# Moving GpSimd's two-tensor instructions to VectorE, and one causal selection for all heads, in a hybrid SSD and short-convolution layer

## The chip, the cores and the metric

The kernel runs on one core of one Trainium2 chip. The metric is the device time of one execution in microseconds; the runs shown are medians of several executions. In the profile PE is the matrix engine (TensorE) and PEld its weight loads, DVE is VectorE, ACT is ScalarE, POOL is GpSimd, and SP is the engine whose queue issues all of this kernel's data DMAs.

## The reference, cut to what matters

One layer on x of 2048 tokens by 1024, in float32:

```python
h = rmsnorm(x, norm_pre)
xbc, dt_raw, z_ssd, sc_h, sc_b, sc_c, z_sc = jnp.split(h @ w_in, idx, axis=-1)
xbc = silu(causal_dwconv(xbc, ssd_conv_w, ssd_conv_b))      # xs, B, C
dt = softplus(dt_raw + dt_bias)
# chunked scan, 16 chunks of 128 tokens, 16 heads in 2 groups
decay_in = exp(segsum(dt * a))                 # exp(acs_l - acs_s) for s <= l, else 0
y_diag = einsum(einsum(C, B) * decay_in, xd)   # C.B^T is shared by a group's 8 heads
states = einsum(B, xd * decay_states)
y_ssd = y_diag + y_off + d_skip * xs
y_ssd = rmsnorm_by_group(y_ssd * silu(z_ssd))
y_sc = sc_b * causal_dwconv(sc_c * sc_h, sc_conv_w) * silu(z_sc)
x = x + rmsnorm(concat(y_ssd, y_sc) @ w_out, norm_post)
out = x + sigmoid(x @ w_ple_gate) * (p @ w_ple_proj)
```

## The kernel before, in words

Everything is kept transposed: channels on the 128 partitions, tokens along the free dimension. The tokens are worked on in two blocks of 1024 (b = 0, 1), each in halves of 512. Precision comes from a split: each float32 operand of a matmul becomes a rounded part (a copy on ACT, L138 for weights and L203 for activations) and the remainder (a subtraction, L139 for weights on VectorE, L204 for activations), and three matmuls stand for one product.

The program has three stages.

**Projection (to about 1069 us).** The input projection is done by a seven-product scheme of the Winograd/Strassen kind (class `Wino`): the weights of two column tiles and the activations of two token halves are added and subtracted first, and seven products p = 1 to 7 take the place of eight. The sums of the weights (`wino_pieces`, L178, L179, L181, L187: tiles `wr_*`) are made on GpSimd. The sums of the activations (`refill`) are made on VectorE or, for some, GpSimd. `Weights.fill` keeps up to six split weight tiles (`ws_*`) ready ahead of PE. Results leave PSUM through ACT (L315) and VectorE (L593, L627, L649, L659, L678); the short convolution's gate ends with two products on GpSimd (L692, L693, tile `vs`). Each block has 13 groups of tiles; from group to group the loads of raw weights (`wr_*`, nine buffers) run ahead.

**Heads (about 1069 to 1384 us).** Eight pairs of head tiles. For a pair: the tokens-by-channels form `px` is made by transposes on PE, multiplied by dt on VectorE (L889, tile `xd`), and that by the decay to the chunk's end on GpSimd (L890, tile `xdd`); the chunk states `pst` need `xdd` (L910). For each of four heads a mask tile `m` (128 x 1024) is filled with the cumulated decays by a broadcast DMA (`m<-acs_d`); GpSimd writes -1e30 where l < s (L936, an affine selection), ACT takes eight exponentials (L939), and VectorE multiplies by `gsb` = C.B^T/4, the same tile for all heads of a group (L941). PE uses the products in `py` (L966) and fills up with matmuls of the second half of the output projection (`os`, L828), 768 in all, dealt out evenly over the steps.

**Output (from about 1384 us).** `out_proj` (PE tile `mo`), post-norm and residual (`residual`: L1080 scales on VectorE, L1081 adds x on GpSimd), then the gate (`mg`, L1104 to L1107). Steps of the norms and of the operands are hung on numbered units by a plan.

The order of the instructions on each engine is fixed when the program is built: a scheduler lays out the instructions by estimated times, so that a change of an engine also changes places on the others. Each engine then takes its own list strictly in order and waits where an operand is late. VectorE makes a part of every split operand and also empties PSUM, so PE can wait for it in two ways.

The lines that the change touches:

```python
G.tensor_tensor(s["e"], s["c"], s["d"], ALU.add)                     # L178, weight sums
(eng or V).tensor_tensor(a[:, 1, :], src, a[:, 0, :].bitcast(F32), ALU.subtract)   # L204
G.tensor_tensor(r4(xdd[gr]), r4(xd[gr]), bc(dst[b]), ALU.mult)       # L890
G.affine_select(m, m, pattern=[[0, NCH], [1, CH]], compare_op=ALU.is_ge, fill=-1e30, ...)   # L936
V.tensor_tensor(mf, mf, s["gsb"][gr], ALU.mult)                      # L941
G.tensor_tensor(x2[d + i], x2[d + i], xk[:, i, :], ALU.add)          # L1081
```

Of the kernel before, what the change touches and what calls it, by code (L numbers as in the profile page):

```python
# [60 lines left out]
def hybrid_kernel(ctx: ExitStack, tc: tile.TileContext, xT, pT, w_t, w_dt, w_o, w_g, w_p, cols_d, cst_d, outT):  # L61
# [99 lines left out]
    def wino_pieces(src, order, pairs, nkk, name, pool):  # L161
# [7 lines left out]
        def fill(p, pr, kk):  # L169
            def f(sp):  # L170
# [4 lines left out]
                elif p == 5:  # L175
                    s["c"], s["d"] = raw(pr, kk, 1, 0), raw(pr, kk, 1, 1)
                    s["e"] = pool.tile([P, 4, P], F32, tag="wraw", name=f"wr_{name}_{label(pr)}_e{kk}")
                    G.tensor_tensor(s["e"], s["c"], s["d"], ALU.add)  # L178
# [21 lines left out]
    def split_act(src, name, p, eng=None, pool=None):  # L200
# [3 lines left out]
        (eng or V).tensor_tensor(a[:, 1, :], src, a[:, 0, :].bitcast(F32), ALU.subtract)  # L204
        return a
# [1002 lines left out]
```

## Time and profile before

| what | value |
|---|---|
| median of 3 runs | 1769.39 us (1767.48 to 1770.1) |
| the profiled execution | 1771.42 us, its span 1769.2 us |
| mean granted PE clock | 0.987 |
| ACT busy | 779.2 us (44%) |
| HBM | 147 GB/s over the span |

The page of a profile gives each engine's busy time; the windows view gives it for stretches that are named; the waits view says which engine stood idle for whom; the timeline lists instructions with their start and length, and in brackets the idle time ahead of one and who ended it. In the profile's instruction names the running numbers of the tiles are left out. Matmul ends are modelled, so PE's busy share is read as "had work", and the rest of a stretch is time in which PE certainly stood.

### The profile page before, as it was taken

Reading aid. Unit: us, or ns where it says so; the run is one execution under the profiler, and the core shown is the slowest. Engines: PE = TensorE matmul, PEld = TensorE weight load, DVE = VectorE, ACT = ScalarE, POOL = GpSimd, SP = SyncE. Lnnn points to the kernel's source line nnn. Section 1 sums busy time; section 2 is a strip of 40 time slices with the busy share of each in tenths; the row PEclk is TensorE's granted clock in tenths of the full one; section 3 lists DMA queues with packets and bytes.
Section 4 is the critical chain, followed back from the end, with each engine's and each line's share of the span. In section 5 each row is a group of like instructions: output and inputs, shape, how many; then the busy total and the mean of one; then the engine's idle time right before and its main releaser. Section 6 shows DMA issues by size and latency. Waiting matters only on the chain. (4 is left out here: it accounts for less than half of the span.)

```text
span 1769.2 us, 23037 instructions
## 1 busy us (share of the span) xinstructions
PE 1678.1 (95%) x8324; PEld 1360.4 (77%) x8324; DVE 1254.9 (71%) x1500; ACT 779.2 (44%) x1408; POOL 627.9 (35%) x450
## 2 busy tenths in 40 slices
PE   7989999989999999999999999998889898998998
PEld 5768878878888788788888887776677686787886
DVE  7986766797669876577766685687578638579632
ACT  7563444435336434344444365455645324152421
POOL 0454243353445543433324443245333104335200
PEclk9999999999999999999999999999999999999999
DMA  9362222673225413221232248687787735435432
GB/s 311 134 202 68 93 83 66 229 250 122 67 66 195 133 60 107 69 84 66 96 107 85 66 155 275 213 262 252 232 261 229 238 105 164 145 119 180 135 119 84
DMA packets 122693, 262.28 MB, mean 148 GB/s; under 512 B 17098, under 2 KB 19658, under 8 KB 121556
## 3 DMA queue, kind: packets, MB, share of 16 engines
q1 hardware_dynamic: 122580, 260.83, 44.9%
q8 instruction: 65, 1.06, 0.3%
q14 instruction: 48, 0.39, 0.1%
HBM read 192.45 MB, written 68.33 MB: 147 GB/s over the span
## 5 line engine op out<-in xcount | busy, mean ns | idle before, releaser
L828 PE MATMUL os<-act_m,ws_os 128*128 128x512 f32 x768 | 191.8, 402 | 3.8 <-ACT po L832 3.2
L214 PE MATMUL mo<-act_m,ws_o 128*128 128x512 f32 x768 | 182.2, 397 | 12.6 <-DVE x L1059 12.6
L214 PE MATMUL mg<-act_x2s,ws_g 128*128 128x512 f32 x768 | 178.5, 394 | 5.8 <-ACT gth L1104 5.8
L214 PEld LDWEIGHTS mo<-act_m,ws_o 128*128 128x128 f32 x768 | 144.8, 190 | 49.9 <-DVE x L1059 12.8
L828 PEld LDWEIGHTS os<-act_m,ws_os 128*128 128x128 f32 x768 | 142.8, 191 | 42.1 <-issue 8.3
L214 PEld LDWEIGHTS mg<-act_x2s,ws_g 128*128 128x128 f32 x768 | 144.1, 189 | 40.0 <-ACT gth L1104 9.8
L139 DVE TENSOR_TENSOR ws_A_gb<-wr_A_gb,ws_A_gb 128x512 fp32r<-128x512 f32 x96 | 89.4, 931 | 35.6 <-ACT ws_A_gb L138 35.4
L204 POOL TENSOR_TENSOR act_m<-mraw,act_m 128x512 fp32r<-128x512 f32 x32 | 53.9, 1688 | 146.9 <-ACT act_m L203 82.7
L138 ACT CAST ws_A_gb<-wr_A_gb 128x512 fp32r<-128x512 f32 x96 | 59.7, 622 | 68.7 <-POOL wr_A_gb L187 20.6
L139 DVE TENSOR_TENSOR ws_A_gc<-wr_A_gc,ws_A_gc 128x512 fp32r<-128x512 f32 x96 | 76.8, 800 | 15.4 <-ACT ws_A_gc L138 14.8
L939 ACT ACTIVATE m<-m,adt 128x128 f32<-128x128 f32 x256 | 77.4, 390 | 16.8 <-POOL m L936 16.8
L606 DVE SCALAR_TENSOR_TENSOR xo<-ux,cols,xo 128x1024 f32<-128x1024 f32 x60 | 80.5, 1344 | 4.5 <-ACT xo L602 4.2
L138 ACT CAST ws_A_gc<-wr_A_gc 128x512 fp32r<-128x512 f32 x96 | 59.8, 623 | 52.7 <-PE A_gc5X L311 8.3
L178 POOL TENSOR_TENSOR wr_A_gc_e<-wr_A_gc,wr_A_gc 128x512 f32<-128x512 f32 x16 | 26.3, 1641 | 138.4 <-DMA wr_A_gc<-in_w_t_dram 119.0
L1105 DVE SCALAR_TENSOR_TENSOR gth<-gth,pe 128x512 f32<-128x512 f32 x32 | 27.5, 859 | 66.8 <-ACT gth L1104 66.8
L1081 POOL TENSOR_TENSOR x<-x,xres 128x512 f32<-128x512 f32 x32 | 50.6, 1600 | 48.8 <-DMA xres<-in_xT_dram 28.5
L1104 ACT ACTIVATE gth<-mg 128x512 f32<-128x512 f32 x32 | 19.1, 598 | 105.4 <-PE mg L214 90.7
L139 DVE TENSOR_TENSOR ws_A_z<-wr_A_z,ws_A_z 128x512 fp32r<-128x512 f32 x48 | 48.2, 1003 | 21.9 <-ACT ws_A_z L138 21.9
L187 POOL TENSOR_TENSOR wr_A_gc<-wr_A_gc,wr_A_gc 128x512 f32<-128x512 f32 x16 | 25.3, 1583 | 103.3 <-DVE ws_A_gc L139 101.4
L936 POOL TENSOR_SCALAR_AFFINE_SELECT m<-m 128x1024 f32<-128x1024 f32 x32 | 47.0, 1478 | 42.2 <-DMA m<-acs_d 41.9
L214 PE MATMUL A_ple<-act_p,ws_p 128*128 128x512 f32 x192 | 49.4, 415 | 11.3 <-ACT ws_p L138 9.1
L890 POOL TENSOR_TENSOR xdd<-xd,dst 128x1024 f32<-128x1024 f32 x16 | 40.3, 2519 | 54.8 <-DVE xd L889 54.8
(504 smaller groups left out, 4070.2 us busy)
## 6 DMA issues: line engine op xcount, KB each, us to landing
wr_A_gc<-in_w_t_dram SPq DMA_DIRECT2D x64, 256.0 KB
wr_A_gb<-in_w_t_dram SPq DMA_DIRECT2D x64, 256.0 KB
m<-acs_d SPq DMA_DIRECT2D x32, 512.0 KB
ple_d<-A_pe SPq DMA_DIRECT2D x32, 256.0 KB
wr_A_xs<-in_w_t_dram SPq DMA_DIRECT2D x32, 256.0 KB
ysc_d<-vs SPq DMA_DIRECT2D x16, 512.0 KB
wr_A_z<-in_w_t_dram SPq DMA_DIRECT2D x32, 256.0 KB
xs_d<-xo SPq DMA_DIRECT2D x16, 512.0 KB
```

The costliest lines, as they stand in the source:

```text
L138: S.copy(sp[:, 0, :kn, :], raw[:, :kn, :])
L139: V.tensor_tensor(sp[:, 1, :kn, :], raw[:, :kn, :], sp[:, 0, :kn, :].bitcast(F32), ALU.subtract)
L178: G.tensor_tensor(s["e"], s["c"], s["d"], ALU.add)
L204: (eng or V).tensor_tensor(a[:, 1, :], src, a[:, 0, :].bitcast(F32), ALU.subtract)
L214: TE.matmul(out, sp[:, a, (k0 + k) % 4, :], act[k0 + k][:, b, :], start=k0 + k == 0 and q == 0, stop=k0 + k == n - 1 and q == 2)
L606: V.scalar_tensor_tensor(o, u[:, q:q + TB], col(w0 + q), o, ALU.mult, ALU.add)
L828: TE.matmul(ps, sp[:, a, k, :], acts_o[tg][KD + kk][:, b_, :], start=kk == 0 and n == 0, stop=kk == KD - 1 and n == 2)
L890: G.tensor_tensor(r4(xdd[gr]), r4(xd[gr]), bc(dst[b]), ALU.mult)
L936: G.affine_select(m, m, pattern=[[0, NCH], [1, CH]], compare_op=ALU.is_ge, fill=-1e30, base=0, channel_multiplier=-1)
L939: S.activation(m[:, c, :], m[:, c, :], AF.Exp, bias=nacs[b][:, h, c:c + 1])
L1081: G.tensor_tensor(x2[d + i], x2[d + i], xk[:, i, :], ALU.add)
L1105: V.scalar_tensor_tensor(th, th, 1.0, pe, ALU.add, ALU.mult)
```

## The change

Every two-tensor instruction that GpSimd did (343: 327 of 128 x 512, 16 of 128 x 1024) is issued on VectorE instead. The 32 selections on the mask tiles are gone. In their place GpSimd selects on `gsb` once per group and block (4 in all), with fill 0, right after ACT has written it; the exponentials then also cover the entries above the diagonal, and the product on VectorE bounds each decay by 1 ahead of the multiplication, in the same instruction. What stays on GpSimd are memsets, small copies and those 4 selections.

```diff
@@ wino_pieces
-                    G.tensor_tensor(s["e"], s["c"], s["d"], ALU.add)
-                    G.tensor_tensor(s["c"], s["c"], s["a"], ALU.subtract)
+                    V.tensor_tensor(s["e"], s["c"], s["d"], ALU.add)
+                    V.tensor_tensor(s["c"], s["c"], s["a"], ALU.subtract)
                     split_w(sp, s["e"])
-                    G.tensor_tensor(s["a"], s["a"], s["e"], ALU.subtract)
+                    V.tensor_tensor(s["a"], s["a"], s["e"], ALU.subtract)
...
-                    G.tensor_tensor(s["a"], s["b"], s["a"], ALU.add)
+                    V.tensor_tensor(s["a"], s["b"], s["a"], ALU.add)
@@ split_act
-        (eng or V).tensor_tensor(a[:, 1, :], src, a[:, 0, :].bitcast(F32), ALU.subtract)
+        V.tensor_tensor(a[:, 1, :], src, a[:, 0, :].bitcast(F32), ALU.subtract)
@@ Wino.refill (and so for p = 6, 7, 4)
-                    e = G if k % 2 and p not in on_v else V
...
-                        e.tensor_tensor(src, t1, t0, ALU.subtract)
+                        V.tensor_tensor(src, t1, t0, ALU.subtract)
@@ prepare
-                G.tensor_tensor(p7, t[:, 1, :], u[:, 1, :], ALU.subtract)
+                V.tensor_tensor(p7, t[:, 1, :], u[:, 1, :], ALU.subtract)
@@ ShortOut.take
-                G.tensor_tensor(v[:, TG:], v[:, TG:], blk[1, 1], ALU.mult)
-                G.tensor_tensor(v[:, :TG], v[:, :TG], z0, ALU.mult)
+                V.tensor_tensor(v[:, TG:], v[:, TG:], blk[1, 1], ALU.mult)
+                V.tensor_tensor(v[:, :TG], v[:, :TG], z0, ALU.mult)
@@ step_g
                     S.activation(s["gsb"][gr], pg[gr], AF.Copy, scale=0.25)
+                    g3 = s["gsb"][gr].rearrange("p (c l) -> p c l", c=NCH)
+                    G.affine_select(g3, g3, pattern=[[0, NCH], [1, CH]], compare_op=ALU.is_ge, fill=0.0, base=0,
+                                    channel_multiplier=-1)
@@ transposes
-                    G.tensor_tensor(r4(xdd[gr]), r4(xd[gr]), bc(dst[b]), ALU.mult)
+                    V.tensor_tensor(r4(xdd[gr]), r4(xd[gr]), bc(dst[b]), ALU.mult)
@@ mask
-                    G.affine_select(m, m, pattern=[[0, NCH], [1, CH]], compare_op=ALU.is_ge, fill=-1e30,
-                                    base=0, channel_multiplier=-1)
                     for c in range(NCH):
                         S.activation(m[:, c, :], m[:, c, :], AF.Exp, bias=nacs[b][:, h, c:c + 1])
                     mf = m.rearrange("p c l -> p (c l)")
-                    V.tensor_tensor(mf, mf, s["gsb"][gr], ALU.mult)
+                    V.scalar_tensor_tensor(mf, mf, 1.0, s["gsb"][gr], ALU.min, ALU.mult)
@@ residual
-                G.tensor_tensor(x2[d + i], x2[d + i], xk[:, i, :], ALU.add)
+                V.tensor_tensor(x2[d + i], x2[d + i], xk[:, i, :], ALU.add)
```

All callers of `split_act` lose their engine argument (`refill`, `p_input`, `later_input`, `mixes_ahead`, `mix_pair`, `operands`). Line numbers of the changed kernel differ by up to two from those before.

How the instructions stand in three places. The last number of a tile's name is a running number and differs between the two programs; the rest is the same tile.

**The heads, third pair.** VectorE before, from the second `ssum` of a pair to the weight splits behind the next pair's masks:

```order
L976 TENSOR_TENSOR ssum_8502<-ssum_8502,gz_9016 128x1024
L941 TENSOR_TENSOR m_9239<-m_9239,gsb_8498 128x1024
L889 TENSOR_TENSOR xd_9329<-px_9320,dts_104 128x1024
L941 TENSOR_TENSOR m_9241<-m_9241,gsb_8498 128x1024
L139 TENSOR_TENSOR ws_os_7_3_9453<-wr_os_7_3_9454,ws_os_7_3_9453 128x512
L139 TENSOR_TENSOR ws_os_0_2_9458<-wr_os_0_2_9459,ws_os_0_2_9458 128x512
```

GpSimd before, at the same place:

```order
L890 TENSOR_TENSOR xdd_9259<-xd_9258,dst_108 128x1024
L936 AFFINE_SELECT m_9239<-m_9239 128x1024
L936 AFFINE_SELECT m_9241<-m_9241 128x1024
L890 TENSOR_TENSOR xdd_9330<-xd_9329,dst_108 128x1024
L936 AFFINE_SELECT m_9308<-m_9308 128x1024
L936 AFFINE_SELECT m_9310<-m_9310 128x1024
```

VectorE with the change:

```order
L977 TENSOR_TENSOR ssum_8502<-ssum_8502,gz_9006 128x1024
L942 SCALAR_TENSOR_TENSOR m_9217<-m_9217,gsb_8498 128x1024
L891 TENSOR_TENSOR xd_9307<-px_9298,dts_104 128x1024
L942 SCALAR_TENSOR_TENSOR m_9219<-m_9219,gsb_8498 128x1024
L892 TENSOR_TENSOR xdd_9308<-xd_9307,dst_108 128x1024
L139 TENSOR_TENSOR ws_os_7_3_9422<-wr_os_7_3_9423,ws_os_7_3_9422 128x512
L139 TENSOR_TENSOR ws_os_0_2_9427<-wr_os_0_2_9428,ws_os_0_2_9427 128x512
```

The selections are gone, and `xdd` stands on VectorE behind `xd`, with one mask product between them. Of the eight pairs' second `xdd`, five stand behind such a product, two behind a weight split, one directly behind `xd`.

**A group's weight sums, projection, first block, after head tiles 2 and 6.** GpSimd before:

```order
L178 TENSOR_TENSOR wr_A_gc_e_3336<-wr_A_gc_100_3332,wr_A_gc_110_3334 128x512
L179 TENSOR_TENSOR wr_A_gc_100_3332<-wr_A_gc_100_3332,wr_A_gc_000_3284 128x512
L604 COPY halo_x<-ux_2_3245 128x3
L178 TENSOR_TENSOR wr_A_gb_e_3364<-wr_A_gb_100_3360,wr_A_gb_110_3362 128x512
L179 TENSOR_TENSOR wr_A_gb_100_3360<-wr_A_gb_100_3360,wr_A_gb_000_3304 128x512
L604 COPY halo_x<-ux_6_3280 128x3
L181 TENSOR_TENSOR wr_A_gc_000_3284<-wr_A_gc_000_3284,wr_A_gc_e_3336 128x512
L181 TENSOR_TENSOR wr_A_gb_000_3304<-wr_A_gb_000_3304,wr_A_gb_e_3364 128x512
L187 TENSOR_TENSOR wr_A_gc_000_3284<-wr_A_gc_010_3465,wr_A_gc_000_3284 128x512
L187 TENSOR_TENSOR wr_A_gb_000_3304<-wr_A_gb_010_3486,wr_A_gb_000_3304 128x512
```

VectorE before, where the results of that group leave PSUM (`ux`, `zo`):

```order
L593 TENSOR_TENSOR ux_2_3245<-A_xs2Z,A_xs_6_3211 128x512
L139 TENSOR_TENSOR ws_A_xs_4_0_3248<-wr_A_xs_110_3011,ws_A_xs_4_0_3248 128x512
L627 TENSOR_TENSOR zo_2_3263<-A_z2Z,A_z_6_3228 128x512
L139 TENSOR_TENSOR ws_A_z_4_0_3265<-wr_A_z_110_3035,ws_A_z_4_0_3265 128x512
L593 TENSOR_TENSOR ux_6_3280<-A_xs2X,A_xs_5_3176 128x512
L139 TENSOR_TENSOR ws_A_gc_1_0_3283<-wr_A_gc_000_3284,ws_A_gc_1_0_3283 128x512
L627 TENSOR_TENSOR zo_6_3300<-A_z2X,A_z_5_3194 128x512
L139 TENSOR_TENSOR ws_A_gb_1_0_3303<-wr_A_gb_000_3304,ws_A_gb_1_0_3303 128x512
```

VectorE with the change:

```order
L139 TENSOR_TENSOR ws_A_xs_4_0_3248<-wr_A_xs_110_3011,ws_A_xs_4_0_3248 128x512
L178 TENSOR_TENSOR wr_A_gb_e_3364<-wr_A_gb_100_3360,wr_A_gb_110_3362 128x512
L179 TENSOR_TENSOR wr_A_gb_100_3360<-wr_A_gb_100_3360,wr_A_gb_000_3304 128x512
L625 TENSOR_TENSOR zo_2_3263<-A_z2Z,A_z_6_3228 128x512
L139 TENSOR_TENSOR ws_A_z_4_0_3265<-wr_A_z_110_3035,ws_A_z_4_0_3265 128x512
L591 TENSOR_TENSOR ux_6_3280<-A_xs2X,A_xs_5_3176 128x512
L139 TENSOR_TENSOR ws_A_gc_1_0_3283<-wr_A_gc_000_3284,ws_A_gc_1_0_3283 128x512
L181 TENSOR_TENSOR wr_A_gc_000_3284<-wr_A_gc_000_3284,wr_A_gc_e_3336 128x512
L625 TENSOR_TENSOR zo_6_3300<-A_z2X,A_z_5_3194 128x512
L139 TENSOR_TENSOR ws_A_gb_1_0_3303<-wr_A_gb_000_3304,ws_A_gb_1_0_3303 128x512
L181 TENSOR_TENSOR wr_A_gb_000_3304<-wr_A_gb_000_3304,wr_A_gb_e_3364 128x512
```

The sums of `wr_A_gb` (which need two loaded raw tiles) now stand in VectorE's list ahead of `zo_2`, the result of PE's tile `A_z2Z`.

**The output stage, between the second reciprocal and the result of `mo_2`.** VectorE before:

```order
L1074 RECIPROCAL rs_1_12213<-rs_1_12213 128x512
L139 TENSOR_TENSOR ws_o_4_0_12264<-wr_o_4_0_12265,ws_o_4_0_12264 128x512
L1080 SCALAR_TENSOR_TENSOR x_0_6_11914<-x_0_6_11914,cols,rs_0_12131 128x512
L1059 TENSOR_TENSOR x_3_1_12240<-mo_0_12179,part_0_12180 128x512
L139 TENSOR_TENSOR ws_o_4_1_12269<-wr_o_4_1_12270,ws_o_4_1_12269 128x512
L1080 SCALAR_TENSOR_TENSOR x_0_7_11949<-x_0_7_11949,cols,rs_0_12131 128x512
L1065 TENSOR_TENSOR ssq_3_12068<-ssq_3_12068,sq_3_1_12242 128x512
L1080 SCALAR_TENSOR_TENSOR x_1_0_11551<-x_1_0_11551,cols,rs_1_12213 128x512
L1080 SCALAR_TENSOR_TENSOR x_1_1_11578<-x_1_1_11578,cols,rs_1_12213 128x512
L1080 SCALAR_TENSOR_TENSOR x_1_2_11691<-x_1_2_11691,cols,rs_1_12213 128x512
L1080 SCALAR_TENSOR_TENSOR x_1_3_11720<-x_1_3_11720,cols,rs_1_12213 128x512
L1059 TENSOR_TENSOR x_2_2_12298<-mo_2_12251,part_2_12252 128x512
```

VectorE with the change:

```order
L139 TENSOR_TENSOR ws_o_3_0_12162<-wr_o_3_0_12163,ws_o_3_0_12162 128x512
L139 TENSOR_TENSOR ws_o_3_1_12167<-wr_o_3_1_12168,ws_o_3_1_12167 128x512
L1081 SCALAR_TENSOR_TENSOR x_0_2_11538<-x_0_2_11538,cols,rs_0_12039 128x512
L1081 SCALAR_TENSOR_TENSOR x_0_3_11567<-x_0_3_11567,cols,rs_0_12039 128x512
L1082 TENSOR_TENSOR x_0_2_11538<-x_0_2_11538,xres_2_12157 128x512
L1082 TENSOR_TENSOR x_0_3_11567<-x_0_3_11567,xres_2_12157 128x512
L139 TENSOR_TENSOR ws_o_4_0_12172<-wr_o_4_0_12173,ws_o_4_0_12172 128x512
L1081 SCALAR_TENSOR_TENSOR x_0_4_11680<-x_0_4_11680,cols,rs_0_12039 128x512
L1081 SCALAR_TENSOR_TENSOR x_0_5_11709<-x_0_5_11709,cols,rs_0_12039 128x512
L1060 TENSOR_TENSOR x_3_1_12148<-mo_0_12087,part_0_12088 128x512
L139 TENSOR_TENSOR ws_o_4_1_12177<-wr_o_4_1_12178,ws_o_4_1_12177 128x512
L1060 TENSOR_TENSOR x_2_2_12206<-mo_2_12159,part_2_12160 128x512
```

The second fence begins three rows behind the reciprocal; in these three stand the result `x_3_0` and one more L1082. Between the reciprocal and the result of `mo_2` stood six scalings (L1080); now four scalings (L1081) and three residual adds (L1082, which were GpSimd's) stand there, and the other scalings come later.

More of the change, by code (lines that the diff above doesn't have):

```diff
@@ L257, in tmp, with refill @@
             return self.pc.tile([P, self.n], F32, tag="wc", name=f"{self.part}_{name}")
-        def refill(self, acts, name, order, l1, l2, on_v=()):
+        def refill(self, acts, name, order, l1, l2):
             h1, h2 = {}, {}
@@ L280, in refill @@
                         src = t0
-                        e.tensor_tensor(src, t0, h2[k, 1], ALU.subtract)
+                        V.tensor_tensor(src, t0, h2[k, 1], ALU.subtract)
                     elif p == 3:
@@ L285, in refill @@
                         src = t1
-                        e.tensor_tensor(src, t1, h2[k, 1], ALU.subtract)
+                        V.tensor_tensor(src, t1, h2[k, 1], ALU.subtract)
                     else:
                         src = h2[k, 0]
-                        e.tensor_tensor(src, src, t0, ALU.add)
-                    acts[p].append(split_act(src, f"{self.part}{name}_{p}{k}", p, e, pact if p in FIRST else self.pactx))
+                        V.tensor_tensor(src, src, t0, ALU.add)
+                    acts[p].append(split_act(src, f"{self.part}{name}_{p}{k}", p, pact if p in FIRST else self.pactx))
                 yield
@@ L420, in p_input @@
                     W.fill(2 * (tg + 1))
-                pa[tg] = [split_act(raws[k], f"p_{tg}{k}", p, None, None if p in FIRST else A.pactx) for k in range(2)]
+                pa[tg] = [split_act(raws[k], f"p_{tg}{k}", p, None if p in FIRST else A.pactx) for k in range(2)]
             for tg in AHEAD:
@@ L450, in l2 @@
                 return h2[k, half]
-            for n, _ in enumerate(A.refill(acts[0], "0", ORDER0, l1, l2, FIRST + (2, 7))):
+            for n, _ in enumerate(A.refill(acts[0], "0", ORDER0, l1, l2)):
                 if 2 <= n < 6:
@@ L501, in later_input @@
                     for i in range(2):
-                        acts[b][p].append(split_act(t[:, i, :], f"A{b}_{p}{k + i}", p, G if k + i == 3 else V,
+                        acts[b][p].append(split_act(t[:, i, :], f"A{b}_{p}{k + i}", p,
                                                     pact if p in FIRST else A.pactx))
@@ L513, in mixes_ahead @@
                     for i in range(2):
-                        acts_o[tg][k + i] = split_act(t[:, i, :], f"m_{tg}_{k + i}", FIRST[2 * tg + (k - KD) // 4],
-                                                      G if i else V)
+                        acts_o[tg][k + i] = split_act(t[:, i, :], f"m_{tg}_{k + i}", FIRST[2 * tg + (k - KD) // 4])
                     if k % 4:
@@ L788, in mix_pair @@
                                        ALU.mult, ALU.mult)
-            acts_o[tg][k + i] = split_act(raw[:, i, :], f"m_{tg}_{k + i}", FIRST[2 * (tg % 2) + k % KD // 4], G if i else V)
+            acts_o[tg][k + i] = split_act(raw[:, i, :], f"m_{tg}_{k + i}", FIRST[2 * (tg % 2) + k % KD // 4])
     def ssd_bank(name):
```

5 lines of the change are left out of this document (2 added, 3 removed).

## The prediction

> **What bounds the kernel now.** I read the page's engine shares first, then a windows view cut where PE's idle time lies, then PE's waits.
>
> ```profile
> PE 1678.1 (95%) x8324; PEld 1360.4 (77%) x8324; DVE 1254.9 (71%) x1500; ACT 779.2 (44%) x1408; POOL 627.9 (35%) x450
> ...
> 37.00:105.00 68.00, 56.73 (x237) 44.78 (x236) 65.21 (x82) 41.32 (x80) 31.96 (x18) 0.95 0.56 187
> ...
> 340.00:400.00 60.00, 54.31 (x235) 43.33 (x234) 54.24 (x56) 25.53 (x42) 28.26 (x19) 1.00 0.72 245
> 400.00:565.00 165.00, 165.00 (x732) 136.45 (x731) 120.25 (x136) 79.15 (x131) 67.03 (x50) 1.00 0.32 106
> 565.00:600.00 35.00, 30.57 (x125) 23.82 (x124) 31.88 (x33) 17.01 (x32) 21.63 (x15) 0.95 0.54 176
> ...
> 1069.00:1384.00 315.00, 283.88 (x2278) 224.43 (x2276) 226.67 (x290) 167.72 (x384) 116.82 (x71) 0.97 0.76 245
> ...
> 1455.00:1520.00 65.00, 53.93 (x223) 42.25 (x222) 56.79 (x63) 21.20 (x35) 24.82 (x16) 0.96 0.51 165
> ...
> 1580.00:1625.00 45.00, 39.87 (x171) 31.70 (x170) 43.98 (x38) 16.45 (x23) 26.56 (x17) 1.00 0.52 164
> ```
>
> A row has the stretch, its length, then busy time and count of PE, PEld, DVE, ACT and POOL, then the granted clock, DMA share and GB/s. PE is the bound over the whole: 1769.2 less 1678.1 leaves 91 us in which it stood. From 400 to 565 it never stands, so nothing on VectorE can gain there, though VectorE has 27% free. PE stands where VectorE is full: in 37:105 VectorE is busy 96%, in 340:400 90%, in 565:600 91%, in 1455:1520 87%, in 1580:1625 98%. PE's idle time there is 11.3 + 5.7 + 4.4 + 11.1 + 5.1 = 37.6 us. In the heads (1069:1384) PE stands 31.1 us with VectorE at 72%: there it is a chain.
>
> ```profile
> PE pst L910 <- POOL xdd L890: 15.1, 8, 5.1
> PE mo L214 <- DVE x L1059: 12.6, 5, 4.1
> ...
> PE A_gc0X L311 <- DVE A_gc L649: 6.7, 1, 6.7
> PE pn L230 <- DVE ssum L976: 6.7, 2, 5.4
> PE mg L214 <- ACT gth L1104: 5.8, 2, 5.1
> ```
>
> PE's waits (total, times, longest) agree: half of the heads' idle time is the eight waits for GpSimd's `xdd`, and in the full stretches PE waits for a PSUM bank that VectorE has not yet emptied.
>
> **Term 1: VectorE's own instructions, with GpSimd beside them and without.** Two engines over the same 6 us of the output stage, where VectorE always has the next instruction ready:
>
> ```profile
> 1490.94 0.68 DVE L1059 TENSOR_TENSOR x<-mo,part 128x512 f32<-128x512 f32 x1
> 1491.55 0.67 DVE L204 TENSOR_TENSOR act_m<-mraw,act_m 128x512 fp32r<-128x512 f32 x1
> 1492.14 1.77 DVE L1080 SCALAR_TENSOR_TENSOR x<-x,cols,rs 128x512 f32<-128x512 f32 x1
> 1493.84 0.68 DVE L1065 TENSOR_TENSOR ssq<-ssq,sq 128x512 f32<-128x512 f32 x1
> 1494.44 1.78 DVE L1080 SCALAR_TENSOR_TENSOR x<-x,cols,rs 128x512 f32<-128x512 f32 x1
> 1496.14 0.68 DVE L139 TENSOR_TENSOR ws_o<-wr_o,ws_o 128x512 fp32r<-128x512 f32 x1
> ...
> 1493.99 1.67 POOL L1081 TENSOR_TENSOR x<-x,xres 128x512 f32<-128x512 f32 x1 [0.63 <-DVE x L1080]
> 1496.30 1.64 POOL L1081 TENSOR_TENSOR x<-x,xres 128x512 f32<-128x512 f32 x1 [0.63 <-DVE x L1080]
> ```
>
> From start to start an undisturbed 128x512 takes VectorE 0.60 us (1491.55 to 1492.14, 1493.84 to 1494.44). The L1080 that runs beside a GpSimd instruction takes 1.70 us (1494.44 to 1496.14). So a GpSimd instruction that meets one of VectorE's costs it 1.1 us, and the same work done by VectorE itself costs 0.60.
>
> By the Trainium skill (SBUF — State Buffer, Who interferes with whom) a VectorE instruction with two SBUF inputs and a GpSimd instruction that reads SBUF exclude each other, and the second waits until the first is done. The trace agrees: 1.70 against 0.60 us.
>
> Not every GpSimd instruction meets one, so I work each full stretch out: VectorE's count there at 0.60 us, plus GpSimd's count (all taken as moved) at 0.60, against the busy time. The reciprocals stand apart:
>
> ```profile
> L1074 DVE RECIPROCAL rs<-rs 128x512 f32<-128x512 f32 x4 | 13.4, 3342 | 0.6 <-ACT rs L1073 0.6
> ```
>
> Two of these four lie in each of the last two stretches (by their timelines). 37:105: 82 x 0.60 + 18 x 0.60 = 60.0, against 65.2: -5.2. 1455:1520: 61 x 0.60 + 6.7 + 16 x 0.60 = 52.9, against 56.8: -3.9. 1580:1625: 36 x 0.60 + 6.7 + 17 x 0.60 = 38.5, against 44.0: -5.5. These three lose 14.6 of 166.0 us, 9%. 340:400 and 565:600 hold 1024-wide instructions as well; at the same 9% of 54.2 + 31.9 they lose 7.6. VectorE's lists in the full stretches become 22 us shorter, though it does more. Not all of PE's idle time there is VectorE's, and a shortened list shows the next cause (ACT, a DMA), so I take two thirds: **-15 us**. The bounds are nothing and all of the 37.6.
>
> In the output stage the order helps too: the adds come off GpSimd's 1.6 us, and the result of `mo_2`, for which PE stands, is moved ahead of two scalings of the other half. That lies within the term.
>
> **Term 2: the heads.** The third pair's second tile, on three engines:
>
> ```profile
> 1165.73 1.22 DVE L889 TENSOR_TENSOR xd<-px,dts 128x1024 f32<-128x1024 f32 x1
> 1166.93 1.23 DVE L941 TENSOR_TENSOR m<-m,gsb 128x1024 f32<-128x1024 f32 x1
> 1168.07 3.92 DVE L139 TENSOR_TENSOR ws_os<-wr_os,ws_os 128x512 fp32r<-128x512 f32 x2
> ...
> 1167.10 2.85 POOL L890 TENSOR_TENSOR xdd<-xd,dst 128x1024 f32<-128x1024 f32 x1 [4.84 <-DVE xd L889]
> ...
> 1170.00 1.20 PE L910 MATMUL pst<-xdd,btok 128*64 128x128 f32 x18 [1.60 <-POOL xdd L890]
> ...
> L936 POOL TENSOR_SCALAR_AFFINE_SELECT m<-m 128x1024 f32<-128x1024 f32 x32 | 47.0, 1478 | 42.2 <-DMA m<-acs_d 41.9
> ...
> L927 DVE SCALAR_TENSOR_TENSOR ea<-ct,ea 128x1024 f32<-128x1024 f32 x16 | 18.8, 1214 | 0.0
> ```
>
> `xd` ends at 1166.95 and PE gets `xdd` at 1170.0, 3.05 later. Changed, one mask product (1.14 from start to start, 1166.93 to 1168.07) and `xdd` at the price of `xd` (1.22) stand there: 2.4, so 0.65 less. Where `xdd` follows `xd` directly it saves 1.6. Ahead of it the chain has the mask, whose product stands in front of `xd` in VectorE's list: without a selection of 1.48 us its exponentials start sooner, though a mask whose DMA lands last gains no more than that. I take 1.1 us of gain for each of the eight waits, together **-9 us**, held by the 15.1 that PE waits for `xdd`. The rest of the 31.1 (loads at a DMA share of 0.76, the `ssum` at the end) I leave as it is. What is late next in this chain is ACT's exponentials and the mask's DMA.
>
> The product with a bound is a form that the trace has only without the bound (L927, 1214 ns mean at 1024 wide, against 1.22 above): nothing either way. The four selections on `gsb` stand several steps ahead of their first reader: nothing; uncovered, 1.48 each, 6 us at the most.
>
> **Term 3: waits that VectorE takes over.** GpSimd stood for data that VectorE now asks for:
>
> ```profile
> POOL wr_A_gc_e L178 <- DMA wr_A_gc<-in_w_t_dram: 119.0, 11, 45.5
> ...
> POOL wr_A_xs_e L178 <- DMA wr_A_xs<-in_w_t_dram: 45.4, 7, 11.0
> ...
> POOL x L1081 <- DMA xres<-in_xT_dram: 28.5, 6, 6.5
> ...
> 403.74 0.68 DVE L627 TENSOR_TENSOR zo<-A_z2Z,A_z 128x512 f32<-128x512 f32 x1
> ...
> 407.04 1.29 POOL L178 TENSOR_TENSOR wr_A_gb_e<-wr_A_gb,wr_A_gb 128x512 f32<-128x512 f32 x1 [1.47 <-DMA wr_A_gb<-in_w_t_dram]
> ```
>
> Most of that is GpSimd being early. But in the changed order the sum of `wr_A_gb` stands ahead of `zo<-A_z2Z`, which ran at 403.74, while its data came at 407.0: VectorE would stand 3.3 us with a PSUM result behind it, then two such results and three weight splits. Such a wait delays PE only if a bank is wanted back within that time; a product of 12 matmuls takes PE 2.7 us (732 in 165 us), eight banks serve it, and six weight tiles lie ready (16 us). I take **+3 us** for the whole. The bounds are nothing, and 20 if half of some 14 groups pass 3 us on to PE.
>
> **The sum.** -15 - 9 + 3 = -21 us. The profiled execution took 1771.4 (span 1769.2), 2 above the median of the runs, 1769.4. So the changed kernel's median is 1748. SP's queue issues the same DMAs, on it only neighbours change places.
>
> **Rivals.**
>
> *Nothing moves (1769, from 1766 to 1773).* PE's idle time is set by ACT and the DMAs, and what VectorE gains becomes their wait. For it: in the heads the DMAs are 76% busy, and the wait for `mg` is put down to ACT. Against it: ACT is 33 to 61% busy in the five full stretches (16.45 of 45 us counts as 37, 21.20 of 65 as 33, 41.32 of 68 as 61), and `mo` and `A_gc0X` wait for VectorE itself.
>
> *VectorE's list is blocked by loads (1780; from 1773 to 1790).* The mechanism of term 3 in the projection, where PE has no slack to give (165.0 of 165): 14 groups x 3.3 us = 46 us of standing VectorE, of which half reaches PE, +23, and with half of the gains, -12: 1769 + 11 = 1780. It decides once a wait is longer than the reserve of a bank, about 5 us (two products). For it: the 119 us row. Against it: VectorE has 45 of 165 us free there.
>
> *VectorE does not become faster (1795).* If its long instructions were long for another reason, the 85 moved instructions of the five stretches (18 + 19 + 15 + 16 + 17) would add 51 us at 0.60 to lists with 3 + 6 + 3 + 8 + 1 = 21 us free: +30, less 4 in the heads. The pairs of 0.68 and 1.78 us above speak clearly against it.
>
> The Trainium skill (Perfetto Trace Analysis, Optimizing Scalar/DVE Operations) advises the opposite for a saturated VectorE, to offload to GpSimd, and adds that between these two it might not help. By the advice this rival's time would come out; the measured 1.70 against 0.60 us decides for the caution.
>
> *More comes free (1730).* All idle time of the full stretches goes (-37.6) and term 2 holds, with term 3 nothing.
>
> **Chances.** The forecast (1735 to 1764) 0.60; more 0.10; nothing moves 0.14; blocked by loads 0.11; not faster 0.05. Some 0.2% (3.5 us) is what a measurement of this kernel can tell from no change. Faster by more: 0.60 + 0.10 = 0.70; same: 0.14; slower: 0.11 + 0.05 = 0.16. The range leaves out the blocked and the not faster case and the far end of "more": 1727 to 1774.
>
> **What would show it.** Term 1: L1080's successor near 0.7 us mean, VectorE's total within 3% of 1255 us despite 343 more instructions, and PE's idle time in the full stretches halved. Term 2: PE's wait for `xdd` below 7 us. Term 3: VectorE's waits for `wr_*` loads under 40 us, with PE still unbroken in the projection. It is wrong if VectorE's total rises by 100 us or more, or if PE waits in the projection where it did not.

## The result, and the profile after

| | before | changed | ratio (95%) |
|---|---|---|---|
| median | 1768.83 us | 1697.48 us (1696.41 to 1702.38) | 0.9602 (0.9582 to 0.9622) |
| span of the profiled execution | 1769.2 us | 1694.7 us | |
| mean granted PE clock | 0.987 | 0.996 | |

The kernel became 4.0% faster, by 71 us. Forecast were 21, and the time lies 30 us below the range's low end of 1727: the sign was right, the size was not.

The page of the changed kernel, engine shares, and below them its windows view. The stretches begin and end with the same matmuls as those shown of before (columns as there; the two stretches that end at 543.20 and 1037.20 answer to 400:565 and to 600:1069):

```profile
PE 1658.7 (98%) x8324; PEld 1351.9 (80%) x8324; DVE 1255.4 (74%) x1843; ACT 783.5 (46%) x1408; POOL 45.6 (3%) x79
```

```profile
37.00:95.70 58.70, 56.84 (x242) 45.75 (x241) 57.40 (x93) 39.37 (x75) 0.00 (x0) 0.98 0.56 185
...
325.40:378.20 52.80, 52.80 (x234) 43.72 (x233) 48.94 (x69) 27.29 (x44) 0.88 (x4) 1.00 0.78 256
378.20:543.20 165.00, 165.00 (x731) 136.50 (x730) 128.96 (x181) 80.41 (x132) 4.08 (x11) 1.00 0.34 116
543.20:571.10 27.90, 27.90 (x124) 23.09 (x123) 25.77 (x41) 16.36 (x28) 7.11 (x2) 1.00 0.62 205
571.10:1037.20 466.10, 466.10 (x2066) 385.91 (x2065) 347.54 (x501) 204.76 (x332) 15.86 (x20) 1.00 0.28 94
1037.20:1326.90 289.70, 276.98 (x2278) 219.94 (x2276) 216.11 (x319) 165.61 (x381) 7.04 (x12) 0.99 0.82 266
...
1399.20:1452.10 52.90, 51.93 (x223) 41.20 (x223) 46.64 (x66) 21.44 (x35) 0.00 (x0) 1.00 0.54 179
...
1512.40:1552.10 39.70, 39.70 (x172) 31.69 (x172) 36.31 (x50) 16.59 (x23) 0.00 (x0) 1.00 0.60 191
```

Three things are to be seen. VectorE does 343 instructions more in the same busy time (1255.4 after 1254.9): what it took over is as much as what it no longer lost. The five full stretches became 41 us shorter (273 to 232), and PE's idle time in them fell from 37.6 to 2.8 us. And PE's busy time fell too, by 19.4 us, though it does the same 8324 matmuls.

The span lost 74.5 us: 34.8 of PE's idle time in the full stretches, 18.4 in the heads (31.1 to 12.7), 1.9 elsewhere, and 19.4 of PE's busy time. The last term is one that the prediction did not have. PE's waits in the changed kernel:

```profile
PE pn L230 <- DVE ssum L977: 4.7, 2, 3.8
PE mo L214 <- DVE x L1060: 4.3, 4, 1.7
...
PE pst L912 <- DVE xdd L892: 0.4, 1, 0.4
```

The 15.1 us for `xdd` are 0.4, the 12.6 for `mo` 4.3, and the 6.7 for `A_gc0X` are gone.

Where PE's busy time went is seen in the kernel before, at a long stand of the output stage. Windows of before; the granted clock is the first number behind POOL's busy time and count:

```profile
1512.20:1516.40 4.20, 0.16 (x1) 0.00 (x0) 4.20 (x6) 0.02 (x1) 2.73 (x2) 0.87 0.74 250
1516.40:1518.00 1.60, 1.56 (x4) 1.31 (x5) 1.60 (x3) 0.61 (x1) 0.41 (x1) 0.50 0.04 8
1518.00:1520.00 2.00, 2.00 (x7) 1.51 (x6) 1.95 (x4) 0.00 (x0) 0.00 (x0) 0.50 0.76 253
1520.00:1522.00 2.00, 2.00 (x6) 1.61 (x5) 0.00 (x0) 0.00 (x0) 1.38 (x2) 0.50 0.01 3
1522.00:1524.00 2.00, 2.00 (x10) 1.56 (x10) 0.00 (x0) 0.00 (x0) 1.14 (x1) 0.96 0.00 0
```

PE stands 4.2 us, and then runs at clock 0.50 for 5.6 us: 17 matmuls start in them, which at the later pace of 10 in 2 us would take 3.4. So this stand cost more than 6 us and not 4.2. In the mean clock: 1769.2 x 0.013 is 23.0 us, 1694.7 x 0.004 is 6.8, a difference of 16.2 of the 19.4, as an estimate.

### The profile page after: what moved, and what is told of

It is laid out like the page before. It is cut to its first block, busy times and chain, and to the rows that moved or that the text cites. A ratio compares the mean times of both kernels' runs of the same rounds, so it can differ in the third digit from the quotient of the medians.

```text
span 1694.7 us, 22635 instructions
## 1 busy us (share of the span) xinstructions
PE 1658.7 (98%) x8324; PEld 1351.9 (80%) x8324; DVE 1255.4 (74%) x1843; ACT 783.5 (46%) x1408; POOL 45.6 (3%) x79
## 4 chain that ended last, share of the span: by engine, by line
PE 85%; DMA 6%; DVE 6%; ACT 2%; issue 1%; SPq 0%; DVEq 0%; ACTq 0%
PE mg L214 10%; PE mo L214 8%; PE os L826 6%; PE py L967 1%; PE A_xs1X L310 1%; PE A_gc6X L310 1%; PE A_gc7X L310 1%; PE A_gb6X L310 1%; PE A_z3X L310 1%; PE A_xs3X L310 1%; PE A_gc5X L310 1%; PE A_z2X L310 1%; PE A_xs2X L310 1%; PE A_gb4X L310 1%; PE A_gc4X L310 1%; PE A_gc3X L310 1%
## 5 line engine op out<-in xcount | busy, mean ns | idle before, releaser
L826 PE MATMUL os<-act_m,ws_os 128*128 128x512 f32 x768 | 186.0, 396 | 2.4 <-ACT po L830 1.7
L826 PEld LDWEIGHTS os<-act_m,ws_os 128*128 128x128 f32 x768 | 141.2, 188 | 37.6 <-issue 6.6
L139 DVE TENSOR_TENSOR ws_A_gb<-wr_A_gb,ws_A_gb 128x512 fp32r<-128x512 f32 x96 | 65.8, 686 | 33.0 <-ACT ws_A_gb L138 32.9
L139 DVE TENSOR_TENSOR ws_A_gc<-wr_A_gc,ws_A_gc 128x512 fp32r<-128x512 f32 x96 | 66.0, 687 | 14.1 <-ACT ws_A_gc L138 12.8
L942 DVE SCALAR_TENSOR_TENSOR m<-m,gsb 128x1024 f32<-128x1024 f32 x32 | 39.6, 1246 | 19.1 <-ACT m L939 16.8
L214 PEld LDWEIGHTS A_ple<-act_p,ws_p 128*128 128x128 f32 x192 | 37.4, 196 | 18.7 <-ACT ws_p L138 9.0
L139 DVE TENSOR_TENSOR ws_A_z<-wr_A_z,ws_A_z 128x512 fp32r<-128x512 f32 x48 | 32.9, 685 | 25.2 <-ACT ws_A_z L138 25.2
L203 ACT CAST act_m<-mraw 128x512 fp32r<-128x512 f32 x64 | 38.1, 621 | 28.9 <-DVE mraw L785 15.8
L138 ACT CAST ws_A_xs<-wr_A_xs 128x512 fp32r<-128x512 f32 x48 | 29.9, 623 | 44.3 <-issue 11.6
L138 ACT CAST ws_A_z<-wr_A_z 128x512 fp32r<-128x512 f32 x48 | 29.9, 623 | 41.9 <-DVE wr_A_z L187 8.6
L1060 DVE TENSOR_TENSOR x<-mo,part 128x512 f32<-128x512 f32 x32 | 22.0, 686 | 29.3 <-PE mo L214 29.3
```

The lines of the kernel that those rows point to most:

```text
L138: S.copy(sp[:, 0, :kn, :], raw[:, :kn, :])
L139: V.tensor_tensor(sp[:, 1, :kn, :], raw[:, :kn, :], sp[:, 0, :kn, :].bitcast(F32), ALU.subtract)
L214: TE.matmul(out, sp[:, a, (k0 + k) % 4, :], act[k0 + k][:, b, :], start=k0 + k == 0 and q == 0, stop=k0 + k == n - 1 and q == 2)
L826: TE.matmul(ps, sp[:, a, k, :], acts_o[tg][KD + kk][:, b_, :], start=kk == 0 and n == 0, stop=kk == KD - 1 and n == 2)
L942: V.scalar_tensor_tensor(mf, mf, 1.0, s["gsb"][gr], ALU.min, ALU.mult)
L1060: V.tensor_tensor(x2[d], ps[:, i, :], pt[:, i, :], ALU.add)
```

## The experiments

Twelve kernels ran. The undoing ones say which part brought what, the first prices the port (what VectorE and GpSimd cost each other when both read SBUF) and the clock by themselves, the last four ask how a longer VectorE list reaches PE. One thousandth of the ratio is 1.8 us.

| run | what | median us | ratio to before (95%) |
|---|---|---|---|
| e2 | head edits undone | 1709.24 | 0.9650 (0.9635 to 0.9664) |
| e3 | weight sums undone | 1715.99 | 0.9691 (0.9677 to 0.9706) |
| e4 | operands and residual undone | 1719.84 | 0.9709 (0.9692 to 0.9725) |
| e5 | rest of the projection undone | 1711.9 | 0.9663 (0.9637 to 0.9689) |
| e6 | only `xdd` undone | 1712.45 | 0.9671 (0.9649 to 0.9692) |
| e7 | only the selections undone | 1705.19 | 0.9638 (0.961 to 0.9666) |
| e8 | head edits alone, on before | 1753.03 | 0.9901 (0.9868 to 0.9934) |
| e9 | 28 more on VectorE, first block | 1709.41 | 0.9657 (0.963 to 0.9684) |
| e10 | 28 more, second block's start | 1717.15 | 0.9691 (0.9667 to 0.9715) |
| e11 | the changed kernel again | 1698.82 | 0.9595 (0.9574 to 0.9617) |
| e12 | 28 more, where there is slack | 1698.66 | 0.9588 (0.9575 to 0.9601) |

### e1: the port and the clock by themselves

```python
phases = [("tt", "", 12, 0), ("", "tt", 0, 6), ("", "copy", 0, 6), ("", "sel", 0, 6),
          ("tt", "tt", 12, 12), ("tt", "copy", 12, 12), ("tt", "sel", 12, 12),
          ("stt", "tt", 12, 12), ("ptt", "", 12, 0), ("ptt", "tt", 12, 12),
          ("copy", "", 12, 0), ("copy", "tt", 12, 12), ("copy", "sel", 12, 12)]
# first VectorE, then GpSimd; "ptt" has one operand in PSUM
```

> The kernel computes nothing of the layer: VectorE runs 12 instructions of 128x512 in a row, alone and with 12 of GpSimd beside them on tiles of its own, in 13 phases that follow each other; then TensorE runs bursts of 60 matmuls (128x512) with a stand of growing length between them. Theory (the two engines exclude each other where both read SBUF): a VectorE instruction with two SBUF operands takes 0.60 us from start to start alone, and 1.6 to 1.9 us while GpSimd's two-tensor instructions run beside it, which take 1.29 us alone and 1.7 or more beside it; with one operand in PSUM it stays at 0.60. A selection or a copy on GpSimd does the same as a sum, 1.3 or more. Rival (they only share bandwidth): 0.7 to 1.0 us in every combination, PSUM operand or not. The stands: theory says that up to 3 us nothing follows, and that from about 4 us on the matmuls behind a stand take twice as long for 3.5 to 5 us, a price of some 2 us each; the rival is that no such step exists and that the lower PE busy time of the changed kernel (1658.7 against 1678.1) comes from something else.

The timeline of this run; the second number is the time of the whole row of equal instructions. L45 is VectorE's sum of two SBUF tiles, L47 the same with one operand in PSUM, L48 a copy; L39, L40, L41 are GpSimd's sum, copy and selection:

```profile
6.47 8.68 DVE L45 TENSOR_TENSOR vo<-va,vb 128x512 f32<-128x512 f32 x12
...
15.75 7.96 POOL L39 TENSOR_TENSOR go<-ga,gb 128x512 f32<-128x512 f32 x6
...
34.01 19.60 POOL L39 TENSOR_TENSOR go<-ga,gb 128x512 f32<-128x512 f32 x12
34.16 20.00 DVE L45 TENSOR_TENSOR vo<-va,vb 128x512 f32<-128x512 f32 x12
...
67.64 11.78 POOL L41 TENSOR_SCALAR_AFFINE_SELECT go<-ga 128x512 f32<-128x512 f32 x12
67.81 12.16 DVE L45 TENSOR_TENSOR vo<-va,vb 128x512 f32<-128x512 f32 x12
...
110.79 16.04 POOL L39 TENSOR_TENSOR go<-ga,gb 128x512 f32<-128x512 f32 x12
110.94 8.67 DVE L47 TENSOR_TENSOR vo<-pv,va 128x512 f32<-128x512 f32 x12
...
127.75 5.50 DVE L48 COPY vo<-va 128x512 f32<-128x512 f32 x12
...
134.00 16.79 DVE L48 COPY vo<-va 128x512 f32<-128x512 f32 x12
```

Alone, VectorE takes 8.68 / 12 = 0.72 us each and GpSimd 7.96 / 6 = 1.33. Beside each other GpSimd takes 19.60 / 12 = 1.63 and VectorE 20.00 / 12 = 1.67. The two work in step, with some overlap: one behind the other they would need 0.72 + 1.33 = 2.05. A pair so costs 1.67 us on two engines, while both on VectorE, one behind the other, would take 2 x 0.72 = 1.45. That is how VectorE's list can become shorter while it gets more instructions. With an operand in PSUM VectorE is not touched (8.67), nor is GpSimd (16.04 / 12 = 1.34). A selection costs VectorE less than expected, 1.01 us each.

The Trainium skill (SBUF — State Buffer, Who interferes with whom) says that a VectorE instruction with at most one SBUF input, outside the two-port modes, does not contend with GpSimd, and that copies can enter those modes and then do; the 8.67 us with a PSUM operand and the copy's 16.79 against 5.50 agree.

The stands, in the same trace. In brackets is how long PE had stood before the 60 matmuls:

```profile
225.27 13.90 PE L72 MATMUL acc<-x,w 128*128 128x512 f32 x60 [2.49 <-ACT x L76]
242.31 16.74 PE L72 MATMUL acc<-x,w 128*128 128x512 f32 x60 [3.14 <-ACT x L76]
262.84 16.71 PE L72 MATMUL acc<-x,w 128*128 128x512 f32 x60 [3.79 <-ACT x L76]
...
306.12 15.65 PE L72 MATMUL acc<-x,w 128*128 128x512 f32 x60 [5.74 <-ACT x L76]
```

Up to a stand of 2.49 us the burst takes 13.9; behind 3.14 and more it takes 15.3 to 16.7. So in this run a stand costs its length, and above some 3 us another 1.4 to 2.8. The Trainium skill (TensorE: Matmul & The Clock Gate, Part 1) has half the clock as the state after an idle window of about 3.4 us, in windows that run freely. Here the step comes earlier, between 2.49 and 3.14 us, and in the kernel before one stand of 2.19 us was followed by half the clock (the last section).

### e2 to e5: one part at a time goes back to GpSimd

```diff
 e2 (heads)
-  V.tensor_tensor(r4(xdd[gr]), r4(xd[gr]), bc(dst[b]), ALU.mult)
+  G.tensor_tensor(r4(xdd[gr]), r4(xd[gr]), bc(dst[b]), ALU.mult)
+  G.affine_select(m, m, ..., fill=-1e30, ...)         # per head, and none on gsb
-  V.scalar_tensor_tensor(mf, mf, 1.0, s["gsb"][gr], ALU.min, ALU.mult)
+  V.tensor_tensor(mf, mf, s["gsb"][gr], ALU.mult)
 e3 (the four kinds of weight sums)
-  V.tensor_tensor(s["e"], s["c"], s["d"], ALU.add)
+  G.tensor_tensor(s["e"], s["c"], s["d"], ALU.add)
 e4 (act_m, x2s, residual)
-  V.tensor_tensor(x2[d + i], x2[d + i], xk[:, i, :], ALU.add)
+  G.tensor_tensor(x2[d + i], x2[d + i], xk[:, i, :], ALU.add)
 e5 (refill, later inputs, p7, the gate's two products)
-  V.tensor_tensor(v[:, TG:], v[:, TG:], blk[1, 1], ALU.mult)
+  G.tensor_tensor(v[:, TG:], v[:, TG:], blk[1, 1], ALU.mult)
```

> The changed kernel with the head edits undone: xdd on GpSimd, a selection on each of the 32 masks there, plain product on VectorE. Theory (the heads' 25 us come from the chain to xdd and from the masks): the stage of the heads gets its 25 us back, the rest keeps its gain: 1722 (1715 to 1728). Rival (the heads are quicker because VectorE is relieved by the other edits, the weight splits above all): less than 8 us come back, 1698 to 1705.

> The changed kernel with the 200 weight sums of the projection on GpSimd again. Theory (port contention in the projection): the stands of the stretches behind 105 us come back, those at 237 to 244, 340 to 400, 565 to 600 and 743 to 750 of before, 22 us with the clock's share, of the 32 that the projection gained: 1719 (1712 to 1723). Rival (the sums on VectorE wait for loads and cost as much as they bring): within 4 us of 1697.

> The changed kernel with the 80 instructions of the operands and of the residual (second half of each split of act_m and x2s, and the adds of x) on GpSimd again. Theory: the output stage gets back its 17 us, and the heads little: 1715 (1709 to 1719). Rival (the order of VectorE's list, not GpSimd's neighbourhood, brought the gain): 1700 to 1706, since the order of the results is mostly kept.

> The changed kernel with the remaining 47 instructions of the projection on GpSimd again (activation sums and their splits in refill and in the later inputs, p7, the two products of the short convolution's gate); the 200 weight sums stay on VectorE. Theory (the parts add up): the projection gave 31.8 us, of which the weight sums took back 17.8 alone, so 14 come back: 1711 (1707 to 1715). Rival (one neighbour less is enough, or 47 instructions are too few to fill VectorE's list): less than 6, 1698 to 1703.

The medians are in the table above. Where the time came back is read from the starts of the same matmuls in the traces, in us: to the last matmul but one of the projection, from there to the 303rd of `mo`, and from there to the last of `mg`. Each row is one profiled execution:

| | projection | heads and start of the output | rest of the output |
|---|---|---|---|
| before | 1069.0 | 386.0 | 308.2 |
| changed | 1037.0 | 362.0 | 289.8 |
| e2 heads back | 1035.8 | 375.4 | 291.2 |
| e3 weight sums back | 1054.1 | 364.8 | 289.6 |
| e4 operands, residual back | 1037.6 | 367.9 | 307.2 |
| e5 rest of projection back | 1046.2 | 361.7 | 290.5 |
| e6 only `xdd` back | 1037.0 | 378.6 | 291.2 |
| e7 only selections back | 1035.5 | 372.4 | 289.7 |
| e8 heads alone, on before | 1069.7 | 367.0 | 307.1 |
| e11 the changed kernel again | 1035.7 | 366.5 | 289.8 |

The changed kernel and e11 are the same program, and their middle column differs by 4.5 us. Differences of that size in this column say nothing.

e3 and e5 came out within the theory's range and e4 just above it: each part returns time in its own stage. Of the projection's 32 us the weight sums return 17 and the rest 9; of the output's 18, operands and residual return 17. The profiled execution of e5 took 1705.97 us and the other three 1711.59 to 1713.93, so its 9 may be too small. Added up by the ratios, the four parts return 0.031 of the 0.040, some 54 of 70 us. What the rest is, parts that gain only together or scatter between runs, stays open.

e3 also shows the price of the port in the kernel itself. The engine shares of its page:

```profile
PE 1666.6 (97%) x8324; PEld 1354.4 (79%) x8324; DVE 1220.5 (71%) x1643; ACT 781.6 (46%) x1408; POOL 337.9 (20%) x279
```

VectorE does 200 instructions fewer than in the changed kernel, 120 us at 0.60 each, and is busy only 35 us less (1220.5 against 1255.4).

e2 fell between both expectations: undoing all head edits returns 13 us of the heads' 24. The other 11 came without the head edits. So the heads' gain was not the chain alone, as I had counted it in the prediction and in this expectation. Which of the other edits brought it is not shown: e4 returns 6 and e3 3 in this column, little more or less than the 4.5 by which the same program differs.

### e6, e7 and e8: the head edits apart

```diff
 e6: of the edits of e2 only xdd on GpSimd (gsb stays selected once)
 e7: of the edits of e2 only the selections on the masks
 e8: the kernel before, with the head edits of the change and nothing else
```

> The changed kernel with only the 16 xdd on GpSimd again, the selection still once on gsb. Theory (the chain to pst is what the heads wait for; with both head edits undone PE waits 9.5 us for xdd): 8 of the 12 us come back, 1705 (1703 to 1708). Rival (the masks make the larger part): 1698 to 1702.

> The changed kernel with the selection on each of the 32 masks on GpSimd again (and the plain product), xdd on VectorE. Theory: 4 of the 12 us come back, 1701.5 (1699 to 1704). Rival (the selection ahead of the exponentials delays the product that stands ahead of xd, and reads SBUF beside VectorE): 8 or more, 1705 to 1709.

> The kernel before with the head edits alone: xdd on VectorE and the selection once on gsb; all other two-tensor work stays on GpSimd. Theory (the parts add up): the 12 to 15 us that the heads lose when they are undone are gained here, 1756 (1753 to 1759). Rival (they need VectorE relieved elsewhere, since xdd adds 19.5 us to it): within 4 of the kernel before, 1766 to 1771.

PE's waits for `xdd`, of e2, of e6 and of e7:

```profile
PE pst L909 <- POOL xdd L889: 9.5, 7, 3.0
```

```profile
PE pst L912 <- POOL xdd L892: 10.3, 7, 2.5
```

```profile
PE pst L909 <- DVE xdd L889: 2.8, 3, 1.9
```

In e2 PE waits 9.5 us for `xdd`, and in the kernel before, with the same head instructions, 15.1. That fits other edits shortening the same wait, though these are single executions.

In the middle column `xdd` alone returns 16.6 us, the selections alone 10.4, both together 13.4. So the two do not add up; that both lie on one chain to `pst`, and that one hides the other, would explain it, but is not shown. That both together return less than `xdd` alone is within the 4.5 us. `xdd` is the larger, as expected, though it cost more than was expected (1712.45 against 1703 to 1708). e7 missed its theory too: 1705.19 lies in the range of its rival, that the selections cost 8 us or more. e8 brought 17.6 us on the kernel before (1770.65 to 1753.03), so the head edits need no relief elsewhere.

### e9, e10, e12: a longer list for VectorE, and e11

The same dose of 28 subtractions that are simply done twice (28 x 0.60 = 17 us for VectorE), in three places of the changed kernel.

```diff
 split_act (e9: called by refill, e10: by the later inputs), split_w (e12: calls 211 to 238)
-  V.tensor_tensor(a[:, 1, :], src, a[:, 0, :].bitcast(F32), ALU.subtract)
+  for _ in range(2):
+      V.tensor_tensor(a[:, 1, :], src, a[:, 0, :].bitcast(F32), ALU.subtract)
```

> The changed kernel in which VectorE does the 28 remainder subtractions of the first block's activations twice (25 of them lie between 37 and 96 us, where VectorE is busy 57.4 of 58.7 us); 28 x 0.60 = 17 us more for VectorE there. Theory (where VectorE's list is full it sets the length of the stretch, one us for one us, and a long stand adds the clock): 16 to 21 us more than the changed kernel of the same call. The prediction's rule (two thirds reach PE): 11. Rival (PE's weights and loads set that stretch): less than 5.

> The same doubling for the 28 remainders of the second block's activations, of which 19 lie between 378 and 543 us, where VectorE is busy 129.0 of 165.0 us, and 9 between 543 and 571, where it is busy 25.8 of 27.9. Theory: nothing from the 19, and from the 9 (5.4 us against 2.1 free) 3 us: 0 to 4 us more than the changed kernel of the same call. Rival (what counts is VectorE's total): the same as the run with the first block's, 16 to 21.

> The changed kernel as it is, beside the two above on the same chip: 0.960 of the kernel before (0.958 to 0.962).

> The changed kernel in which VectorE does 28 of the weight splits' subtractions twice, those between about 590 and 670 us, where each 20 us of the changed kernel have VectorE busy for 12.9 to 18.5 us, some 24 us free in all; 17 us more for VectorE, as in the two runs before, in which the list had no gap and all 17 us reached PE. Theory (PE pays only for what the list cannot take in locally): nothing, the stretch from 570 to 755 us as long as in the changed kernel, the whole within 3 us of it. Rival (VectorE's total counts, or a longer way from raw weight to split delays PE): 11 to 18 us more.

Windows of e9, from 37 us to one matmul of `A_gc0X`, and of e11 to the same matmul:

```profile
37.00:112.40 75.40, 62.59 (x258) 48.22 (x257) 73.81 (x120) 40.82 (x78) 0.00 (x0) 0.98 0.42 146
```

```profile
37.00:94.90 57.90, 55.89 (x241) 45.12 (x240) 56.36 (x91) 39.50 (x76) 0.00 (x0) 0.99 0.55 186
```

VectorE's busy time grew by 17.45 us, and that matmul came 17.5 us later. But PE was not held up for all of it: in the longer window it does 17 matmuls more (258 against 241), which belong to the groups behind (`A_gc1X`, `A_gb1X`) and were laid ahead of this one. Where both programs have done the same matmuls again, one of `A_gb1X` starts 13.0 us later. So 13.0 of 17.45 us, three quarters, reached PE. The total grew by 10.6, less than the 16 to 21 that I had expected and about what two thirds would give; its scatter (1704.46 to 1720.09 us in six executions) is too wide to tell one from the other.

e10 missed its expectation wholly, +18.3 us where 0 to 4 stood. Windows of e10, and of e11 for the same matmuls:

```profile
542.00:587.10 45.10, 34.94 (x125) 26.99 (x124) 42.18 (x68) 18.18 (x32) 9.50 (x2) 0.85 0.51 166
```

```profile
520.00:540.00 20.00, 20.00 (x90) 16.57 (x89) 20.00 (x31) 16.59 (x31) 0.10 (x1) 1.00 0.77 255
...
541.70:569.60 27.90, 27.90 (x125) 23.10 (x124) 25.42 (x40) 16.23 (x28) 7.09 (x2) 1.00 0.61 197
```

The place was not free. I had taken VectorE's share from 378 to 543 us (129 of 165); but from 520 to 540 VectorE is busy 20.00 of 20 us in the changed kernel, so that what is added there has to be done later. VectorE's busy time in the last stretch grew by 16.8 us and the stretch by 17.2: one for one. PE does the same 125 matmuls in it; it stood for 10.2 us, and the other 7.0 are busy time, at a clock of 0.85. The profiled execution of e10 took 1710.97 us where the median is 1717.15; its middle column, which this edit leaves alone, is 358.2 against 366.5 us in e11. So the stretch is a firmer reading than the total.

In e12 the same dose lies where VectorE has local slack. Windows of e12 and of e11:

```profile
590.00:670.00 80.00, 80.00 (x355) 66.24 (x354) 70.09 (x105) 31.46 (x52) 6.62 (x3) 1.00 0.20 70
```

```profile
590.00:670.00 80.00, 80.00 (x355) 66.24 (x354) 56.36 (x81) 33.58 (x53) 1.66 (x3) 1.00 0.22 79
```

VectorE works 13.7 us more in these 80, PE never stands, and the total is that of the changed kernel (1698.66 against 1698.82).

No run points to a version faster than the changed kernel: each part that went back cost time, the selections (e7) the least.

## Why the prediction was right in sign and wrong in size

**The bound: right.** The five stretches that were named, and the heads, gave 66 of the 74.5 us.

**VectorE's total: right.** Forecast was a total within 3% of 1255 us in spite of 343 more instructions; it is 1255.4. The scaling of the output stage takes 744 ns in the mean (it was 1170), as forecast near 0.7 us. e1 shows the mechanism by itself.

**From VectorE's list to PE's idle time: the step that failed.** The prediction shortened the lists of the full stretches by 22 us and let two thirds reach PE, -15. In fact the lists became 37 us shorter (252.1 to 215.1 us, by the five rows above), and PE's idle time there fell by 34.8. Both factors were off.

The 22 us assumed that every moved instruction stays in its stretch. But the two engines together have 32 instructions fewer in the five stretches (357 to 325, by the counts of the rows), worth 19 us at 0.60. Most of them stand in neighbouring stretches that had room: 9 more in the one behind 37:105, 14 in the one behind 1455:1520, 6 in 400:565. The first two, before and then with the change:

```profile
105.00:340.00 235.00, 232.87 (x1016) 191.18 (x1017) 168.80 (x211) 98.74 (x163) 90.24 (x77) 0.98 0.32 106
...
1520.00:1580.00 60.00, 60.00 (x257) 48.38 (x256) 30.15 (x38) 22.28 (x37) 20.98 (x15) 0.98 0.38 123
```

```profile
95.70:325.40 229.70, 228.94 (x1017) 188.60 (x1016) 181.48 (x275) 102.43 (x171) 10.15 (x22) 1.00 0.35 119
...
1452.10:1512.40 60.30, 58.69 (x256) 47.54 (x255) 42.98 (x67) 22.34 (x37) 0.00 (x0) 1.00 0.45 144
```

The discount of a third had no number behind it. Its reason was that a shortened list shows the next cause; none showed, PE's idle time in the five stretches is 2.8 us. Added work passes on nearly all where the list has no gap and PE nothing else to do (e10: 17.2 us for 16.8), three quarters where PE has other matmuls ahead (e9), and nothing where the list has slack (e12).

**No term for the clock: the second failure.** The sum took PE's 1678.1 us of busy time as fixed. It fell by 19.4 us, and by the mean clock some 16 of these are the clock's. e1 shows the price of a stand, the windows of before and of e10 show it in the kernel; stand by stand the 19.4 us were not added up. The rows that would have told stood in the prediction: the clock column read 0.95 for 37:105, 0.97 for the heads, 0.96 for 1455:1520.

**The heads: right in mechanism, -9 against -25.** PE's wait for `xdd` went nearly whole (15.1 to 0.4), where 1.1 us for each of the eight had been taken. 6.9 us of the stage are PE's busy time, with the clock at 0.97 before and 0.99 after. And the prediction priced nothing that the other edits bring in the heads: without the head edits (e2) the middle column still became 10.6 us shorter (386.0 to 375.4). How these parts overlap stays open.

**Waits that VectorE takes over: forecast +3, measured nothing.** VectorE does wait for loads now; the longest such row of the changed kernel:

```profile
DVE wr_A_gb_e L178 <- DMA wr_A_gb<-in_w_t_dram: 12.3, 14, 2.7
```

With the others (5.3 for `wr_A_gc`, 3.6 for `wr_A_z`) it is about 21 us, below the 40 of the forecast, and PE is unbroken in the two long stretches of the projection (165.0 of 165.0 and 466.1 of 466.1 us). The rival of a blocked list did not come about: the waits seem to fall into VectorE's slack, as the added work of e12 did.

**The rival "more comes free" (1730)** was the nearest. It took all idle time of the full stretches, and still missed the clock and half of the heads. Its own terms give 1769.4 - 37.6 - 9 = 1723, not 1730; that lies below the range's low end as well.

## What to carry to other kernels

Cut the profile until each stretch is either full or slack for the engine that feeds PE: here a shorter list counted almost whole in the full ones (34.8 of 37 us), added work not at all in a slack one, and a mean over a long stretch hid which it was. Look also at where the instructions will stand afterwards, and not only at what each costs. Price a stand of PE by the clock behind it as well as by its length; the clock column of the windows view shows it. Two engines that hold each other up are worth less than one if the pair takes longer than both jobs in a row on the faster engine: 1.67 us against 1.45 here.
